# A hybrid recurrent and attention layer: two gate tiles ahead of the pairs, the bias of the first heads in a buffer of its own, the causal mask by GpSimd's select

## The chip, the cores and the metric

The kernel runs on one core of one Trainium2 chip. Its engines are TensorE (PE in the profile, with the weight loads as PEld), VectorE (DVE), ScalarE (ACT), GpSimd (POOL) and SyncE (SP), which only issues transfers. Each takes its own instructions in order and waits on semaphores for the others. The metric is the device time of one execution in microseconds (us); lower is better.

## The reference

One layer of a streaming encoder on 512 tokens of width 1024, all in float32. The part that matters here:

```python
proj = h @ w_in                      # xa, ga, q, k, v, f, gA, gB
y_a = gelu(ga) * rg_lru(conv(xa))    # recurrent branch, width 1280
cum = cumsum(log_sigmoid(f + b_forget))            # one row for each of 16 heads
sc = q @ k.T / 8 + cum[:, None] - cum[None, :]     # in blocks of 128 queries
sc = where(key <= query, sc, -inf)                 # causal mask
y_b = softmax(sc) @ v                              # width 1024
merged = sigmoid(gA + bA) * (y_a @ P_A) + sigmoid(gB + bB) * (y_b @ P_B)
x = x + norm(merged @ w_out)                       # then the feed-forward part
```

The eight column tiles of 128 of `gA` are called ma0 to ma7 in the kernel and those of `gB` mb0 to mb7. The feed-forward part after it (`up` and `dn` in the profile) is not touched by the change.

## The kernel before

Every float32 product is made of three matmuls of rounded parts: each operand is split into a high part, a cast by ScalarE, and a low part, the remainder by VectorE (`wh` and `wl` of a weight, `hh` and `hl` of the normed input, `h_q` and `l_q` of a projection). `mm3` (line 218) issues the three, and `project` (223) makes one tile of 128 output channels by 512 tokens of 24 such matmuls.

The stages stand one behind the other: input norm and `xa`, `v`, the recurrent branch with `ga`, the product `pa` (y_a times P_A), the gates, attention, `pb` (y_b times P_B) with the merge, `wo`, and the feed-forward part. The weights that are fetched one tile at a time stand in the list `order` (186 to 199). `unit(name, ahead)` takes the tile of that name and, ahead of that, emits load (SP's queue), cast and subtraction of all tiles up to `ahead` places behind it. All raw, high and low weight tiles come from one pool with four buffers of each kind (94).

Of the gates, ma0 to ma7 and mb0 to mb5 are made in seven pairs of tiles by a scheme that saves multiplications (`Pair`, 333, and `period`, 431), which needs sums of weight parts (`gt`, `gth`, `gtl`, pool `gsum`), plain parts (`gmh`, `gml`, pools `gsplit0` and `gsplit1`) and kept partial results (`gx`, pool `gkeep`). A low plain part is made by ScalarE's negated copy and an adding transfer from GpSimd's queue (354). mb6 and mb7 are plain projections (`gate_tile`, 869): mb6 stands ahead of the pairs (883), mb7 in attention's last iteration (1071). Each gate's tanh is used at once (ma) or stored to DRAM in `gmb` (mb, 867) and loaded again for the merge.

Attention runs over eight pairs of heads p (1064). An iteration issues, in this order, the scores of pair p, the projection q of pair p + 1, the transposes `pt` of the probabilities of pair p - 1, the projection k of pair p + 1, the halves of q and k, and the product `av` of pair p - 1 with the values; then the division of pair p. In the first iteration there is no `pt` and no `av`; in the last one mb7 stands in the place of q and `pb_part(0, ...)` in that of k. Behind the loop follow `pt` and `av` of the last pair, with parts of pb0, pb1 and pb2 between them (1084 to 1088). `pb_part(e, ks)` adds the steps ks of tile pb e, three matmuls each; step k needs `yb[k]`, the result of `av` of pair k.

The scores of a head need its bias row, which `prep_alloc` (953) fetches: a transfer from GpSimd's queue spreads the row `cnd[h]`, which lies in DRAM since the `pa` stage, over 128 partitions of a tile `B` (957), and two adding transfers put the mask of 128x128, `maskf`, onto its four diagonal blocks (960). VectorE adds scores and bias and takes the extreme of each row (990), ScalarE takes the exponential (995), VectorE divides (1005). `B` has two buffers, one for each head of a pair, so the fetch for pair p + 1 waits until the scores of pair p have been read. `B`, `maskf` and all other tiles of attention lie in the pool `attn`, opened behind the gates over the place of `gsum` and `gkeep`.

PSUM has eight banks (96). The scores of a pair take six, `pt` six, `av` two, every projection and every open pb tile one.

The order of the instructions is the text's between `tc.manual_schedule()` (890) and the end of the gates' block. Elsewhere a planner with estimated times may issue a later instruction first when an earlier one would wait. Memory is taken over from closed pools; with `reuse_waits="tile"` an instruction waits only for the old tiles under its own.

Of the kernel before, what the change touches and what calls it, by code (L numbers as in the profile page):

```python
# [63 lines left out]
def kernel(  # L64
# [115 lines left out]
    def cols(w, i):  # L180
        return w[i], (KD, P)
# [7 lines left out]
    order += [(f"pa{e}_{i}", w_pa[2 * e + i], (5, P)) for e, i in PA_ORDER]  # L189
    order.append(("mb6", *cols(w_in, B_MB + 6)))  # L190
    for p in range(KD):
        order.append((f"q{p}", *cols(w_in, B_Q + p)))
        order.append((f"k{p}", *cols(w_in, B_K + p)))
    order.append(("mb7", *cols(w_in, B_MB + 7)))
    order += [(f"pb{e}", *cols(w_pb, e)) for e in range(KD)]
# [276 lines left out]
    with ExitStack() as rg:  # L472
# [336 lines left out]
        dstk = mstk.enter_context(ExitStack())  # L809
        hfstk = ExitStack()  # L810
        fq = []

        def early_sums(step):
            if step == 3:
                forget()
                rg2.close()
                gates.tpool = dstk.enter_context(tc.tile_pool(name="gsum", bufs=2, reuse_waits="tile"))
                gates.kpool = dstk.enter_context(tc.tile_pool(name="gkeep", bufs=2, reuse_waits="tile"))
                hfpool = hfstk.enter_context(tc.tile_pool(name="hf", bufs=1, reuse_waits="tile"))
                fq.extend(hfpool.tile([P, KH, SH], F32, name=f"hf{i}") for i in range(4))  # L820
            elif 6 <= step < 10:
                i = step - 6
                k, c = (slice(0, KH), slice(KH, KD))[i % 2], (X, Y)[i // 2]
                dve.tensor_tensor(out=fq[i], in0=hh[:, k, c].bitcast(F32), in1=hl[:, k, c].bitcast(F32), op=ALU.add)
            elif step == 10:
                dve.tensor_tensor(out=fq[3], in0=fq[2], in1=fq[3], op=ALU.add)
                sub(fq[2], fq[0], fq[2])
            elif step == 11:
                sub(fq[0], fq[3], fq[0])
                sub(fq[1], fq[1], fq[0])  # L830
            elif step == 12:
                gp[0] = Pair(gates, 0, GP[0])
            elif step == 13:
                gp[0].sums(0)
                gp[0].sums(1)
            elif step == 14:
                gp[0].sums_hi(0)
                gp[0].sums_lo(0)
            elif step == 15:
                gp[0].sums_hi(1)  # L840
                gp[0].sums_lo(1)
# [40 lines left out]

    gate_tile("mb6", 0)
    with ExitStack() as g2:
# [9 lines left out]
        hfstk.close()  # L894
        st0pool = g2.enter_context(tc.tile_pool(name="gsplit0", bufs=2, side="right", reuse_waits="tile"))
        offset(g2, 448, "right")
        st1pool = g2.enter_context(tc.tile_pool(name="gsplit1", bufs=2, side="right", reuse_waits="tile"))
        gates.stpools = [st0pool, st1pool]
# [27 lines left out]
        for j in range(len(GP)):  # L926
            period(gp[j], gp.get(j - 1), gp.get(j + 1, none), gp.get(j + 2, none), gate_epilogue, lambda: more(j))
            gp.pop(j - 1, None)
        b = gp.pop(len(GP) - 1)
        b.add(b.c[:, Y], b.a[:, Y], 1)  # L930
# [9 lines left out]
        gate_epilogue(b, "a", 1)  # L940
    dstk.close()

    with ExitStack() as at:
        apool = at.enter_context(tc.tile_pool(name="attn", bufs=2, reuse_waits="tile"))

        maskf = apool.tile([P, P], F32, name="maskf", bufs=1)
        pool.memset(maskf, 0.0)
        pool.affine_select(
            out=maskf, in_=maskf, compare_op=ALU.is_ge, fill=NEG, base=0,
            pattern=[[-1, P]], channel_multiplier=1)  # L950
        mask2 = maskf.rearrange("p (a b) -> p a b", a=1).to_broadcast([P, 2, P])

        def prep_alloc(p):
            bias = []
            for h in (2 * p, 2 * p + 1):
                B = apool.tile([P, PO[NT]], F32, tag="B", name=f"B{h}")
                nc.gpsimd.dma_start(B, cnd[h : h + 1, :].partition_broadcast(P))
                for c0, w, o in ((0, 256, 0), (256, 512, 384)):
                    diag = B[:, c0 : c0 + 2 * w].rearrange("p (a b) -> p a b", a=2)[:, :, o : o + P]
                    nc.gpsimd.dma_start(diag, mask2, accum_op=ALU.add)  # L960
                bias.append(B)
            return bias

# [96 lines left out]

        bias = prep_alloc(0)
        q, k = halves(pq, "q0"), halves(pk, "k0")
        prev = None
        for p in range(KD):
# [5 lines left out]
            else:  # L1070
                gate_tile("mb7", 2)
            if prev is not None:
# [5 lines left out]
            else:  # L1078
                pb_part(0, range(KD - 2))
            if prev is not None:  # L1080
# [3 lines left out]
        pts = pt(KD - 1, prev)  # L1084
        pb_part(1, range(KD - 1))
        av(KD - 1, pts)
        pb_part(0, range(KD - 2, KD - 1))
        pb_part(2, range(KD - 1))

# [10 lines left out]
    def tg_load(e):  # L1100
        if e < KD:
            tgs[e] = tgpool.tile([P, S], F32, tag="tg", name=f"tg{e}")
            nc.sync.dma_start(tgs[e], gmb[e])

    for e in range(2):
        tg_load(e)
# [559 lines left out]
```

## Time and profile before

| what | value |
| --- | --- |
| time, median of 3 runs | 937.4 us (936.6 to 939.69) |
| profiled execution | 937.35 us |
| span of its profile | 935.6 us |
| instructions | 15714 |
| mean granted TensorE clock | 0.994 |
| DMA | 191.27 MB, mean 204 GB/s |

The span runs from the first to the last instruction of the profiled execution; 1.75 us of its time lie around it. A row of a timeline gives start and duration in us, engine, line, operation, the tile written and the tiles read, shapes and count; in brackets the idle time of the engine just ahead of it and what ended that. A row of waits gives engine, tile and line that waited, what it waited for, the total in us, the number of times and the longest. A row of a window gives its bounds, its length, busy time and instructions of TensorE, the granted clock as a share of full speed, the mean busy share of the DMA engines and GB/s. In the names, numbers of buffers are left out: mb6 and mb7 are both `mb`.

### The profile page before, as it was taken

Reading aid. Unit: us, or ns where it says so; the run is one execution under the profiler, and the core shown is the slowest. Engines: PE = TensorE matmul, PEld = TensorE weight load, DVE = VectorE, ACT = ScalarE, POOL = GpSimd, SP = SyncE. Lnnn points to the kernel's source line nnn. Section 1 sums busy time; section 2 is a strip of 40 time slices with the busy share of each in tenths; the row PEclk is TensorE's granted clock in tenths of the full one; section 3 lists DMA queues with packets and bytes.
Section 4 is the critical chain, followed back from the end, with each engine's and each line's share of the span. In section 5 each row is a group of like instructions: output and inputs, shape, how many; then the busy total and the mean of one; then the engine's idle time right before and its main releaser. Section 6 shows DMA issues by size and latency. Waiting matters only on the chain.

```text
span 935.6 us, 15714 instructions
## 1 busy us (share of the span) xinstructions
PE 911.4 (97%) x5834; PEld 803.7 (86%) x5834; DVE 724.7 (77%) x1184; ACT 596.9 (64%) x1033; POOL 243.1 (26%) x252
## 2 busy tenths in 40 slices
PE   8999999999989997999999999999999999999996
PEld 7988888878889985788888889999999999978885
DVE  5866369537967446888876678999999999889897
ACT  7555495433467535677663376687888888676664
POOL 4134335434121123423303200033232323100001
PEclk9999999999999998999999999999999999999999
DMA  7667589989687586757743555088988989699764
GB/s 276 218 224 206 161 233 261 252 212 199 162 213 182 151 256 167 182 147 187 163 180 130 196 180 182 17 201 219 230 231 211 225 223 205 220 367 328 235 205 143
DMA packets 80320, 191.27 MB, mean 204 GB/s; under 512 B 7729, under 2 KB 36193, under 8 KB 79858
## 3 DMA queue, kind: packets, MB, share of 16 engines
q1 hardware_dynamic: 47360, 127.33, 40.8%
q0 software_dynamic: 32592, 62.40, 32.2%
q8 instruction: 46, 0.75, 0.3%
q10 hardware_dynamic: 290, 0.53, 0.1%
q14 instruction: 32, 0.26, 0.1%
HBM read 150.69 MB, written 35.73 MB: 199 GB/s over the span
## 4 chain that ended last, share of the span: by engine, by line
PE 84%; DMA 7%; DVE 3%; issue 3%; POOL 1%; ACT 1%; SPq 0%; DVEq 0%; POOLq 0%; ACTq 0%
PE up L406 6%; PE up L409 6%; PE up L407 6%; PE dn L1390 4%; PE dn L1388 4%; PE dn L1389 4%; DMA B<-maskf 2%; PE ga L221 2%; PE ga L220 2%; PE ga L219 2%; PE pa L220 2%; PE pa L219 2%; PE pa L221 2%; PE pb L219 2%; PE wo L1129 2%
## 5 line engine op out<-in xcount | busy, mean ns | idle before, releaser
L354 POOL DMA_DIRECT2D ml<-raw_up x41 | 35.1, 857 | 158.7 <-ACT mh L362 75.7
L1274 DVE SCALAR_TENSOR_TENSOR u<-up,cpt,u 128x511 f32<-128x511 f32 x96 | 71.2, 744 | 2.6 <-ACT u L1268 0.9
L1390 PE MATMUL dn<-wh_dn,al 128*128 128x512 f32 x168 | 65.7, 391 | 0.8 <-DVE al L318 0.8
L1388 PE MATMUL dn<-wh_dn,ah 128*128 128x512 f32 x168 | 65.5, 390 | 0.1
L1389 PE MATMUL dn<-wl_dn,ah 128*128 128x512 f32 x168 | 65.4, 389 | 0.0
L406 PE MATMUL up<-sh,th 128*128 128x256 f32 x252 | 60.6, 277 | 1.6 <-DVE up L425 1.1
L407 PE MATMUL up<-sl,th 128*128 128x256 f32 x252 | 60.4, 276 | 0.0
L175 DVE TENSOR_TENSOR wl_dn<-raw_dn,wh_dn 128x1024 fp32r<-128x1024 f32 x42 | 51.5, 1226 | 9.3 <-ACT wh_dn L172 9.2
L172 ACT CAST wh_dn<-raw_dn 128x1024 fp32r<-128x1024 f32 x42 | 44.1, 1049 | 17.7 <-issue 11.5
L318 DVE TENSOR_TENSOR tl<-t,th 128x1024 fp32r<-128x1024 f32 x42 | 51.1, 1218 | 2.5 <-ACT th L388 2.5
L1282 POOL TENSOR_TENSOR yf<-u,u 128x512 f32<-128x512 f32 x24 | 32.2, 1341 | 69.4 <-issue 43.5
L406 PEld LDWEIGHTS up<-sh,th 128*128 128x128 f32 x252 | 47.3, 188 | 2.0 <-DVE up L425 1.3
L995 ACT ACTIVATE P<-P,mx 128x384 f32<-128x384 f32 (+2 forms) x64 | 35.2, 552 | 20.7 <-DVE mx L990 19.8
L388 ACT CAST th<-t 128x1024 fp32r<-128x1024 f32 x42 | 43.8, 1044 | 6.3 <-DVE t L318 4.0
L960 POOL DMA_DIRECT2D B<-maskf x32 | 39.2, 1756 | 31.6 <-DMA B<-cnd 31.3
L407 PEld LDWEIGHTS up<-sl,th 128*128 128x128 f32 x252 | 47.3, 188 | 0.0
L1268 ACT ACTIVATE u<-up,cpt 128x512 f32<-128x512 f32 x48 | 37.0, 779 | 16.2 <-PE up L409 8.8
L406 PE MATMUL up<-h2h,mh 128*128 128x256 f32 x168 | 40.2, 276 | 0.0
L407 PE MATMUL up<-h2l,mh 128*128 128x256 f32 x168 | 40.2, 276 | 0.0
L1390 PEld LDWEIGHTS dn<-wh_dn,al 128*128 128x128 f32 x168 | 31.5, 188 | 8.6 <-DVE al L318 2.1
L409 PE MATMUL up<-sh,tl 128*128 128x256 f32 x252 | 38.9, 276 | 0.0
L353 ACT ACTIVATE ml<-raw_up 128x512 fp32r<-128x512 f32 (+1 forms) x41 | 34.2, 833 | 6.6 <-DMA raw_up<-in_w_up_dram 6.6
(718 smaller groups left out, 3275.1 us busy)
## 6 DMA issues: line engine op xcount, KB each, us to landing
raw_up<-in_w_up_dram SPq DMA_DIRECT2D x48, 512.0 KB, 5.4
td<-in_w_down_dram POOLq DMA_DIRECT2D x36, 512.0 KB, 6.1
raw_dn<-td SPq DMA_DIRECT2D x24, 512.0 KB, 5.1
B<-cnd POOLq DMA_DIRECT2D x16, 640.0 KB, 5.1
ml<-raw_up POOLq DMA_DIRECT2D x20, 512.0 KB, 5.2
raw_dn<-in_w_down_dram SPq DMA_DIRECT2D x18, 512.0 KB, 3.7
raw_wo<-in_w_out_dram SPq DMA_DIRECT2D x16, 512.0 KB, 3.6
td<-td POOLq DMA_DIRECT2D x12, 512.0 KB, 10.9
```

The lines of the kernel that those rows point to most:

```text
L172: act.copy(self.wh, self.raw)
L175: engine.tensor_tensor(out=self.wl, in0=self.raw, in1=self.wh.bitcast(F32), op=ALU.subtract)
L219: pe.matmul(dst, ah, bh, start=first, stop=False)
L318: dve.tensor_tensor(out=out, in0=a, in1=b, op=ALU.subtract)
L388: act.copy(self.th[i], self.t[i])
L406: pe.matmul(dst, wh[:, k], ah[:, k], start=first and k == 0, stop=False, skip_group_check=True)
L407: pe.matmul(dst, wh[:, k], al[:, k], start=False, stop=False, skip_group_check=True)
L409: pe.matmul(dst, wl[:, k], ah[:, k], start=False, stop=k == KH - 1, skip_group_check=True)
L1274: dve.scalar_tensor_tensor(out=c[:, s:], in0=ps[:, : S - s], scalar=col(C_CFW + 3 * e + j), in1=c[:, s:], op0=ALU.mult, op1=ALU.add)
L1388: pe.matmul(dst[t], ah[:, k, tok], wh[:, k], start=first, stop=False, skip_group_check=True)
L1389: pe.matmul(dst[t], ah[:, k, tok], wl[:, k], start=False, stop=False, skip_group_check=True)
L1390: pe.matmul(dst[t], al[:, k, tok], wh[:, k], start=False, stop=last, skip_group_check=True)
```

## The change

Four things are changed. mb7 moves in `order` and in the text from attention's last iteration to right behind mb6, ahead of the pairs. The bias tiles get a pool of their own, `bias`, with two buffers, opened behind the pairs' loop in the place of `gsum` (which is now above `gkeep` and closed early, as are the pools of the split parts), and the first pair's `prep_alloc` is issued there, ahead of the last additions, q0 and k0. The mask is no longer a tile added by transfers: GpSimd's `affine_select` puts -1e30 into the upper half of each of the four diagonal blocks of a bias tile, in place. And in the tail pb0's first six steps take mb7's place, pb1's first six those of pb0; the seventh steps of both follow the last `pt`, then pb2's first seven, and then the last `av`. `gkeep` stays open until the merge.

```diff
--- before.py
+++ after.py
@@ -187,11 +187,10 @@
     order += [(f"v{c}_{u}", w_in[B_V + 4 * c + u], (2, 512)) for c in range(2) for u in range(4)]
     order += [(f"ga{t}", *cols(w_in, B_GA + t)) for t in range(TR)]
     order += [(f"pa{e}_{i}", w_pa[2 * e + i], (5, P)) for e, i in PA_ORDER]
-    order.append(("mb6", *cols(w_in, B_MB + 6)))
+    order += [(f"mb{e}", *cols(w_in, B_MB + e)) for e in (6, 7)]
     for p in range(KD):
         order.append((f"q{p}", *cols(w_in, B_Q + p)))
         order.append((f"k{p}", *cols(w_in, B_K + p)))
-    order.append(("mb7", *cols(w_in, B_MB + 7)))
     order += [(f"pb{e}", *cols(w_pb, e)) for e in range(KD)]
     for ph in range(2):
         order += [(f"wo{ph}_{k}", *rows(w_out, k)) for k in range(KD)]
@@ -807,15 +806,15 @@
         GP = [(f"{w}{e}", f"{w}{e + 1}") for w, n in (("ma", 8), ("mb", 6)) for e in range(0, n, 2)]
         gp = {}
         dstk = mstk.enter_context(ExitStack())
-        hfstk = ExitStack()
+        sumstk, hfstk, splitstk, bstk = (ExitStack() for _ in range(4))
         fq = []
 
         def early_sums(step):
             if step == 3:
                 forget()
                 rg2.close()
-                gates.tpool = dstk.enter_context(tc.tile_pool(name="gsum", bufs=2, reuse_waits="tile"))
                 gates.kpool = dstk.enter_context(tc.tile_pool(name="gkeep", bufs=2, reuse_waits="tile"))
+                gates.tpool = sumstk.enter_context(tc.tile_pool(name="gsum", bufs=2, reuse_waits="tile"))
                 hfpool = hfstk.enter_context(tc.tile_pool(name="hf", bufs=1, reuse_waits="tile"))
                 fq.extend(hfpool.tile([P, KH, SH], F32, name=f"hf{i}") for i in range(4))
             elif 6 <= step < 10:
@@ -880,7 +879,21 @@
             else:
                 gate_use(name, b.tg[which])
 
-    gate_tile("mb6", 0)
+    def prep_alloc(p):
+        bias = []
+        for h in (2 * p, 2 * p + 1):
+            B = bpool.tile([P, PO[NT]], F32, tag="B", name=f"B{h}")
+            nc.gpsimd.dma_start(B, cnd[h : h + 1, :].partition_broadcast(P))
+            bias.append(B)
+        for B in bias:
+            for b in (3, 2, 1, 0):
+                diag = B[:, PO[b + 1] - P : PO[b + 1]]
+                pool.affine_select(out=diag, in_=diag, compare_op=ALU.is_ge, fill=NEG, base=0,
+                                   pattern=[[-1, P]], channel_multiplier=1)
+        return bias
+
+    gate_tile("mb6", 1)
+    gate_tile("mb7", 0)
     with ExitStack() as g2:
         spool = g2.enter_context(tc.tile_pool(name="gsums", bufs=1, side="right", reuse_waits="tile"))
         gates.sh = [spool.tile([P, KH, SH], F32R, name=f"gsh{i}") for i in range(4)]
@@ -892,9 +905,9 @@
             act.copy(gates.sh[i], f)
             sub(gates.sl[i], f, gates.sh[i].bitcast(F32))
         hfstk.close()
-        st0pool = g2.enter_context(tc.tile_pool(name="gsplit0", bufs=2, side="right", reuse_waits="tile"))
-        offset(g2, 448, "right")
-        st1pool = g2.enter_context(tc.tile_pool(name="gsplit1", bufs=2, side="right", reuse_waits="tile"))
+        st0pool = splitstk.enter_context(tc.tile_pool(name="gsplit0", bufs=2, side="right", reuse_waits="tile"))
+        offset(splitstk, 448, "right")
+        st1pool = splitstk.enter_context(tc.tile_pool(name="gsplit1", bufs=2, side="right", reuse_waits="tile"))
         gates.stpools = [st0pool, st1pool]
         none = Nothing()
         p, n = gp[0], gp[1]
@@ -926,6 +939,10 @@
         for j in range(len(GP)):
             period(gp[j], gp.get(j - 1), gp.get(j + 1, none), gp.get(j + 2, none), gate_epilogue, lambda: more(j))
             gp.pop(j - 1, None)
+        splitstk.close()
+        sumstk.close()
+        bpool = bstk.enter_context(tc.tile_pool(name="bias", bufs=2, reuse_waits="tile"))
+        bias = prep_alloc(0)
         b = gp.pop(len(GP) - 1)
         b.add(b.c[:, Y], b.a[:, Y], 1)
         b.add(b.c[:, X], b.c[:, X], 0)
@@ -938,28 +955,10 @@
         b.product(4, b.a[:, Y])
         gate_epilogue(b, "a", 0)
         gate_epilogue(b, "a", 1)
-    dstk.close()
 
     with ExitStack() as at:
+        at.enter_context(bstk)
         apool = at.enter_context(tc.tile_pool(name="attn", bufs=2, reuse_waits="tile"))
-
-        maskf = apool.tile([P, P], F32, name="maskf", bufs=1)
-        pool.memset(maskf, 0.0)
-        pool.affine_select(
-            out=maskf, in_=maskf, compare_op=ALU.is_ge, fill=NEG, base=0,
-            pattern=[[-1, P]], channel_multiplier=1)
-        mask2 = maskf.rearrange("p (a b) -> p a b", a=1).to_broadcast([P, 2, P])
-
-        def prep_alloc(p):
-            bias = []
-            for h in (2 * p, 2 * p + 1):
-                B = apool.tile([P, PO[NT]], F32, tag="B", name=f"B{h}")
-                nc.gpsimd.dma_start(B, cnd[h : h + 1, :].partition_broadcast(P))
-                for c0, w, o in ((0, 256, 0), (256, 512, 384)):
-                    diag = B[:, c0 : c0 + 2 * w].rearrange("p (a b) -> p a b", a=2)[:, :, o : o + P]
-                    nc.gpsimd.dma_start(diag, mask2, accum_op=ALU.add)
-                bias.append(B)
-            return bias
 
         def halves(ps, name):
             hi = apool.tile([P, S], F32R, tag=f"{name[0]}h", name=f"h_{name}", bufs=1)
@@ -1058,7 +1057,6 @@
             for k in ks:
                 mm3(pb[e], wh[:, k], wl[:, k], yb[k][:, 0], yb[k][:, 1], k == 0, k == KD - 1)
 
-        bias = prep_alloc(0)
         q, k = halves(pq, "q0"), halves(pk, "k0")
         prev = None
         for p in range(KD):
@@ -1068,7 +1066,7 @@
                 pq = bank(f"q{p + 1}")
                 project(pq, unit(f"q{p + 1}"), hh, hl)
             else:
-                gate_tile("mb7", 2)
+                pb_part(0, range(KD - 2))
             if prev is not None:
                 pts = pt(p - 1, prev)
             if p < KD - 1:
@@ -1076,16 +1074,16 @@
                 project(pk, unit(f"k{p + 1}"), hh, hl)
                 q, k = halves(pq, f"q{p + 1}"), halves(pk, f"k{p + 1}")
             else:
-                pb_part(0, range(KD - 2))
+                pb_part(1, range(KD - 2))
             if prev is not None:
                 av(p - 1, pts)
             normalise(now)
             prev = now
         pts = pt(KD - 1, prev)
-        pb_part(1, range(KD - 1))
+        for e in range(2):
+            pb_part(e, range(KD - 2, KD - 1))
+        pb_part(2, range(KD - 1))
         av(KD - 1, pts)
-        pb_part(0, range(KD - 2, KD - 1))
-        pb_part(2, range(KD - 1))
 
     ustk = ExitStack()
     h2pool = ustk.enter_context(tc.tile_pool(name="h2T", bufs=1, side="right", reuse_waits="tile"))
@@ -1102,6 +1100,7 @@
             tgs[e] = tgpool.tile([P, S], F32, tag="tg", name=f"tg{e}")
             nc.sync.dma_start(tgs[e], gmb[e])
 
+    dstk.close()
     for e in range(2):
         tg_load(e)
     for e in range(KD):
```

## Prediction

> **What bounds the kernel now.** I read the page first, the share of each engine:
>
> ```profile
> PE 911.4 (97%) x5834; PEld 803.7 (86%) x5834; DVE 724.7 (77%) x1184; ACT 596.9 (64%) x1033; POOL 243.1 (26%) x252
> ```
>
> TensorE is busy 97% of the span of 935.6 us, so a change that leaves its matmuls as they are can gain at most its idle stretches and the time at a lower clock. The waits of TensorE, longest first, say where these lie:
>
> ```profile
> PE s2c L981 <- ACT h_k L967: 4.5, 1, 4.5
> PE ma L409 <- DMA gml<-raw_ma: 1.7, 1, 1.7
> PE ma L406 <- DVE ma L425: 1.3, 1, 1.3
> PE s4c L981 <- DVE l_k L968: 1.0, 1, 1.0
> PE ma L406 <- ACT gmh L362: 0.4, 1, 0.4
> ```
>
> Two places count. The gates' first pair (the ma rows) waits 0.4 + 1.3 + 1.7 = 3.4 us. Attention's first pairs (the rows s2c and s4c) wait 5.5 us, and more is lost there, since the granted clock falls with the idleness. The windows of TensorE, with granted clock behind the busy time:
>
> ```profile
> 354.00:362.00 8.00, 4.76 (x26) 0.57 0.86 229
> 388.00:475.00 87.00, 87.00 (x643) 1.00 0.66 163
> ```
>
> From 388 to 475 us, the rest of attention, it never idles: nothing is to be gained there. The wait of 4.5 us is put down to ScalarE's cast h_k. The chain of waits says what held that up (start, us, what):
>
> ```profile
> 333.25 13.31 DMA B<-maskf
> ```
>
> and the timelines of GpSimd, VectorE and ScalarE show the order:
>
> ```profile
> 316.99 0.55 POOL L957 DMA_DIRECT2D B<-cnd  x1 [2.68 <-DVE gtl L318]
> 317.55 0.31 POOL L948 TENSOR_SCALAR_AFFINE_SELECT maskf<-maskf 128x128 f32<-128x128 f32 x1
> 331.64 0.57 POOL L957 DMA_DIRECT2D B<-cnd  x1 [13.78 <-DVE mb L425]
> 341.62 1.19 POOL L960 DMA_DIRECT2D B<-maskf  x1 [6.66 <-DMA B<-cnd]
> 346.73 0.69 DVE L990 CUSTOM_DVE_ANT_0 P<-s0c,B 128x512 f32<-128x512 f32 x1 [5.72 <-DMA B<-maskf]
> 356.52 0.58 ACT L967 CAST h_k<-k 128x512 fp32r<-128x512 f32 x1
> ```
>
> The second head's bias is issued only at 331.64, since its buffer overlaps what the gates' last addition reads. The adding transfers of the mask take 13.31 us to land. So VectorE reads the first scores at 346.73, the exponentials follow, and ScalarE, which works in order, casts the next k at 356.52, long after its projection.
>
> **The change part by part.** *mb7 ahead of the pairs.* Attention's iterations, by the starts of their first matmuls:
>
> ```profile
> 341.47 0.50 PE L219 MATMUL q<-hh,wh_q 128*128 128x512 f32 x1
> 382.33 0.50 PE L219 MATMUL q<-hh,wh_q 128*128 128x512 f32 x1
> 399.71 0.50 PE L219 MATMUL q<-hh,wh_q 128*128 128x512 f32 x1
> 405.38 0.28 PE L1017 MATMUL pt<-ident,P 64*128 64x64 f32 x2
> 406.77 0.50 PE L219 MATMUL k<-hh,wh_k 128*128 128x512 f32 x1
> 412.34 0.39 PE L1041 MATMUL av<-PTh,v 128*128 128x512 f32 x1
> 414.91 0.50 PE L981 MATMUL s8c<-h_k,h_q 64*128 64x512 f32 x1
> 417.11 0.50 PE L219 MATMUL q<-hh,wh_q 128*128 128x512 f32 x1
> ```
>
> A projection of 24 matmuls, q here and mb7 in the last iteration, takes 405.38 - 399.71 = 5.67 us. Those of mb7 leave attention and stand behind mb6: nothing in the sum of the matmuls. There they run beside the gates' start:
>
> ```profile
> 259.86 0.37 ACT L413 COPY gx<-ma 128x256 f32<-128x256 f32 x1 [2.02 <-PE ma L409]
> 260.66 0.42 DVE L425 TENSOR_TENSOR ma<-ma,gx 128x256 f32<-128x256 f32 x1
> 258.13 0.69 DVE L318 TENSOR_TENSOR gt<-raw_ma,raw_ma 128x512 f32<-128x512 f32 x1
> 448.20 1.23 DVE L175 TENSOR_TENSOR wl_pb<-raw_pb,wh_pb 128x1024 fp32r<-128x1024 f32 x1 [2.03 <-ACT wh_pb L172]
> ```
>
> The 5.67 us cover the wait for the cast (0.4) and for the gml transfer (1.7) even when mb7's own cast and subtraction (of the form of wl_pb, 1.23) go ahead of them on ScalarE and VectorE. Of the 1.3 the chain matmul, copy (0.37), addition (0.42), matmul stays, some 0.9 with its hand-overs; 0.4 goes, in which VectorE finished a sum first. Gain 0.4 + 1.7 + 0.4 = **2.5 us**, with 1.5 (the moved work collides) and 3.4 (all of it) as ends. mb7's load joins SP's queue between mb6's and the first pair's successors; the four raw buffers then come free one load later for the second raw_ma. It is first read at 258.13, and TensorE needs the result 5.67 us later than now: covered. Its tanh and its store to gmb join ScalarE and SP with the others; behind that store wait the next loads of gate weights, which have as much cover.
>
> *First heads' bias, and the mask by select.* 32 adding transfers, maskf and its two GpSimd instructions go. 64 selects of 128x128 come, eight for each pair, and the first two bias loads are issued in the gates' stage. They lie over the sums' buffers, whose last reader let GpSimd go at 316.99; one may touch a buffer of the plain parts, which the last pair's product 3 reads shortly ahead of q0. The load of 331.64 landed 10 us later, at 341.62. At that rate both land by some 327, and eight selects end well ahead of the first use, 346.73 - 5.72 = 341.0: that wait goes, and with it what follows. The loads share the queues with k0's weights; q0's projection, 5.67 us, covers these. On GpSimd nothing is queued behind the selects but the next bias loads. Attention's other tiles lie 16 KB higher, over splits and sums of the gates that are read for the last time ahead of q0: no wait. The size follows from the starts above. An undisturbed iteration takes 417.11 - 399.71 = 17.40 us, of which pt is 406.77 - 405.38 = 1.39 and av 414.91 - 412.34 = 2.57. The iteration of pair 0 (its q projection starts at 341.47) has neither: 13.44 us. But av is what covers the casts of k in the others:
>
> ```profile
> 447.14 0.39 PE L1041 MATMUL av<-PTh,v 128*128 128x512 f32 x1
> 448.07 0.58 ACT L967 CAST h_k<-k 128x512 fp32r<-128x512 f32 x1
> 449.34 0.68 DVE L968 TENSOR_TENSOR l_k<-k,h_k 128x512 fp32r<-128x512 f32 x1
> ```
>
> From the end of the projection (447.14) h_k takes until 448.65, 1.5 us, and l_k until 450.02, 2.9 us. So a wait remains ahead of pair 1's scores, 1.5 and then 0.6 behind the matmuls that need h_k alone: 2.1 us. Pairs 0 and 1 then take 13.44 + 2.1 + 17.40 = 32.9 us, against 382.33 - 341.47 = 40.86 now. Gain **7.9 us**; 10.0 if independent matmuls fill the remaining wait, 6 if the selects delay pair 1 by some 2 us.
>
> What the selects cost in the other pairs: the only one in the trace took 0.31, beside an idle VectorE. What a GpSimd instruction costs in contention, the small copies show (min/median/max in ns), and what VectorE runs most in attention:
>
> ```profile
> L149 POOL COPY tick<-wh_v x8: 1170/1171/1172, 60.2 to 114.5; 128x1 f32<-128x1 f32 x8
> L149 POOL COPY tick<-wh_xa x5: 178/187/1172, 32.2 to 52.0; 128x1 f32<-128x1 f32 x5
> 390.16 4.88 POOL L960 DMA_DIRECT2D B<-maskf  x4 [3.53 <-DMA B<-cnd]
> 399.79 0.69 DVE L990 CUSTOM_DVE_ANT_0 P<-s7c,B 128x512 f32<-128x512 f32 x1
> ```
>
> The same copy of 128x1 takes 0.19 or 1.17 us: up to 0.98 more when it is held. A select lies between 0.31 and 1.29; I take 0.5, nearer the select's own row. The first bias of a pair has landed at 390.16 and the second is read at 399.79: 9.6 us for eight selects that need 4, in place of adding transfers with their landing. Cost nothing; VectorE loses at most 8 x 0.31 = 2.5 us in an iteration of 17.4.
>
> The Trainium skill speaks against this part: its page "SBUF — State Buffer", section "Who interferes with whom", has GpSimd and VectorE share one pair of ports that is held for a whole instruction, so that a GpSimd instruction that reads SBUF and a VectorE instruction with two SBUF inputs, or in a two-port mode, block each other. By that rule each select may wait for a whole subtraction of attention's weights; the copies' two durations agree with it, and what it would make of the time is the slower rival below.
>
> *pb in the tail.* The same 192 pb matmuls in another order. mb7's place is filled by pb0 (18 matmuls), pb0's by pb1. But pb2 now stands ahead of the last av, and the first matmuls written behind that av need its result:
>
> ```profile
> 358.41 0.79 PE L219 MATMUL q<-hh,wh_q 128*128 128x512 f32 x1
> 483.15 0.28 PE L1017 MATMUL pt<-ident,P 64*128 64x64 f32 x2
> 483.87 0.69 DVE L1046 TENSOR_TENSOR y<-av,ytmp 64x512 f32<-64x512 f32 x1 [0.53 <-ACT ytmp L1045]
> 485.25 0.69 DVE L1049 TENSOR_TENSOR yb<-y,yb 128x512 fp32r<-128x512 f32 x1
> 492.03 0.45 PE L219 MATMUL pb<-yb,wh_pb 128*128 128x512 f32 x1
> 494.23 0.69 DVE L1049 TENSOR_TENSOR yb<-y,yb 128x512 fp32r<-128x512 f32 x1 [0.69 <-ACT yb L1048]
> ```
>
> The last av ends at 492.03 and its yb is there at 494.92: 2.9 us, now covered by 24 pb matmuls. After the change they are covered only if pb3's matmuls, ready and later in the text, are issued first; such a lift happens already (the q matmul of 358.41 stands among pair 1's scores). Ahead of it the last pt needs six banks while pb0, pb1 and av's two are held: the last comes free when y is read (484.56, 1.4 us behind pt's start), about 0.8 us of wait. And pb0's step 6 follows pt at once, where yb comes at 485.94, 2.8 us behind av against pt's 1.46: some 0.5 more. Full price 2.9 + 0.8 + 0.5 = 4.2; nothing if all is lifted; I take **+1.2**.
>
> Sum: -2.5 - 7.9 + 1.2 = -9.2. The profiled execution took 937.35 us, the median is 937.4: **928.2 us**.
>
> **The rivals.** *The tail waits in full*: +4.2 instead of +1.2 gives 931.2. For it: the order of the text; against it: the lifted q matmul. *The first bias comes late all the same* (the change doesn't do what it says): the new buffer waits for another tile or the load lands behind its neighbours. Then pair 0's wait stays, and of attention's gain only pair 1's late part goes: s4c's 1.0, and in the chain one landing of adds; some 3 of 7.9, so 933. Against it: even the load of 331.64, landed at 341.62 without the queue of adds behind it, would beat 346.73. *Selects partly held*, 1.29 each: 8 x 1.29 = 10.3 from 390.16 ends at 400.5, 0.7 late in each of seven iterations, 5 us: 933. *Selects held by every subtraction* (the other side): 0.31 + 1.23 = 1.54 each ends at 390.16 + 12.3 = 402.5, 2.7 us behind the read at 399.79, seven times, 19 us: 947, slower. It decides from about 1.36 us a select, where 8 x 1.36 - 9.6 = 1.3 us an iteration eats the 9.2. Against it: the select's own 0.31, and that an iteration has only two such subtractions.
>
> **How the numbers follow.** Forecast 0.57 (its own range 924 to 931), tail in full 0.15, late bias 0.05, selects partly held 0.07; two of these together, some 936, 0.07; selects held throughout 0.09. A measurement of this kernel tells about 0.3%, 2.8 us, from no change: faster 0.84, same 0.07, slower 0.09. The range reaches from all gains at their upper ends (3.4 + 10.0, no cost: 924, and 0.5 for the scatter) to the first four cases with their scatter: 923.5 to 935.
>
> **What would show it.** Right: no wait at ma rows but about 0.9; h_k of pair 1 within 2 us of its projection; clock 1.00 from 354 to 362; the s8c to q marks still 17.4 apart. Wrong: selects above 1.2 us, a wait of VectorE on them in the later pairs, TensorE idle behind the last av, or a wait ahead of k0's projection since the early bias loads share the queues with its weights.

## The result and the profile after

The changed kernel takes 925.43 us (median of 4 runs, 924.3 to 925.92), the kernel before 937.0 (936.49 to 939.69) beside it: a ratio of 0.9869, with a 95% interval of 0.9848 to 0.9891. The page of its profile begins:

```profile
span 923.2 us, 15775 instructions
PE 907.4 (98%) x5834; PEld 802.3 (87%) x5834; DVE 722.3 (78%) x1184; ACT 598.3 (65%) x1033; POOL 222.0 (24%) x282
```

The matmuls are as many as before; the span is 12.4 us shorter (935.6 - 923.2), of which TensorE is busy 4.0 us less and idle 8.4 us less. The waits of TensorE that answer to those of the prediction:

```profile
...
PE s2c L980 <- ACT h_k L966: 1.4, 1, 1.4
PE ma L405 <- DVE ma L424: 0.9, 1, 0.9
...
PE pt L1016 <- DVE y L1045: 0.4, 1, 0.4
```

The 4.5 us ahead of pair 1's scores (s2c) are 1.4, those ahead of pair 2's (s4c) are gone, and of the gates' 3.4 us the 0.9 of one chain is left. One wait of 0.4 is new, in the tail. The two windows of before, with busy time and granted clock of TensorE:

```profile
354.00:362.00 8.00, 6.61 (x43) 1.00 0.39 138
388.00:475.00 87.00, 87.00 (x644) 1.00 0.40 140
```

The clock in the first is 1.00 where it was 0.57; the second never idled and doesn't now. What the clock is worth shows in the windows from the first matmul of s0c to that of s4c, pairs 0 and 1 of attention, before and after:

```profile
338.56:378.98 40.42, 34.63 (x202) 0.92 0.71 188
```

```profile
341.37:374.50 33.13, 31.15 (x201) 1.00 0.58 201
```

Of the 7.29 us that this stretch gains, 3.81 are idle time (5.79 before, 1.98 after) and 3.48 are busy time, for the same matmuls at a granted clock of 1.00 instead of 0.92: the lower clock cost nearly as much as the waits. To see where the time came from, take from the timelines of TensorE the first matmul of each stage, before:

```profile
254.44 0.28 PE L406 MATMUL ma<-gsh,gth 128*128 128x256 f32 x1
...
326.06 0.39 PE L219 MATMUL q<-hh,wh_q 128*128 128x512 f32 x1
...
338.56 0.50 PE L981 MATMUL s0c<-h_k,h_q 64*128 64x512 f32 x1
...
378.98 0.49 PE L981 MATMUL s4c<-h_k,h_q 64*128 64x512 f32 x1
...
397.51 0.50 PE L981 MATMUL s6c<-h_k,h_q 64*128 64x512 f32 x1
...
467.11 0.50 PE L981 MATMUL s14c<-h_k,h_q 64*128 64x512 f32 x1
...
526.79 0.39 PE L1129 MATMUL wo<-wh_wo,mh 128*128 128x512 f32 x1
```

and after:

```profile
260.71 0.28 PE L405 MATMUL ma<-gsh,gth 128*128 128x256 f32 x1
...
328.87 0.39 PE L218 MATMUL q<-hh,wh_q 128*128 128x512 f32 x1
...
341.37 0.50 PE L980 MATMUL s0c<-h_k,h_q 64*128 64x512 f32 x1
...
374.50 0.50 PE L980 MATMUL s4c<-h_k,h_q 64*128 64x512 f32 x1
...
391.88 0.50 PE L980 MATMUL s6c<-h_k,h_q 64*128 64x512 f32 x1
...
461.42 0.50 PE L980 MATMUL s14c<-h_k,h_q 64*128 64x512 f32 x1
...
516.58 0.39 PE L1128 MATMUL wo<-wh_wo,mh 128*128 128x512 f32 x1
```

Their differences, in us, for these two and for the experiments below (`pa` to `ma` is the stage ahead, into which mb7's projection has gone; `up` to `dn` is the feed-forward part, which no kernel of the table alters):

| profile | pa-ma | ma-q | q-s0c | s0c-s4c | s4c-s6c | s6c-s14c | s14c-wo | up-dn |
| --- | --- | --- | --- | --- | --- | --- | --- | --- |
| before | 63.55 | 71.62 | 12.50 | 40.42 | 18.53 | 69.60 | 59.68 | 237.92 |
| after | 69.02 | 68.16 | 12.50 | 33.13 | 17.38 | 69.54 | 55.16 | 236.33 |
| bias and select alone (e1) | 63.57 | 73.07 | 12.50 | 33.18 | 17.38 | 69.53 | 59.69 | 236.41 |
| gate tile and tail alone (e2) | 68.98 | 68.17 | 12.50 | 40.72 | 18.57 | 69.57 | 56.30 | 236.35 |
| select, bias as before (e4) | 68.99 | 68.16 | 12.50 | 33.20 | 17.38 | 69.55 | 55.17 | 238.21 |
| early bias, mask added (e3b) | 69.08 | 68.20 | 16.48 | 33.18 | 17.96 | 69.55 | 55.14 | 236.89 |
| each select three times (e5) | 69.02 | 68.32 | 12.50 | 36.72 | 17.38 | 69.88 | 55.19 | 236.45 |
| each select six times (e6) | 68.99 | 68.27 | 12.51 | 37.31 | 27.53 | 96.13 | 61.65 | 236.31 |
| three steps of q2 first (e7) | 69.07 | 68.16 | 12.50 | 31.64 | 17.42 | 69.52 | 55.20 | 236.55 |
| after, with the old tail (e8) | 69.00 | 68.18 | 12.57 | 33.14 | 17.37 | 69.46 | 55.52 | 236.36 |

From before to after: gates -3.46, attention's start -7.29 and -1.15, mb7 leaving attention and entering the gates, with the tail, 5.47 - 4.52 = +0.95. That is -10.95 of the 12.4. The rest is in stages that the change doesn't touch: -1.59 from `up` to `dn` (which varies from 236.3 to 238.2 over the table), +0.80 ahead of `pa`, and -0.66 in sum elsewhere.

The timelines of GpSimd, VectorE and ScalarE show how attention starts now:

```profile
319.80 0.55 POOL L886 DMA_DIRECT2D B<-cnd  x1 [6.86 <-DVE gtl L317]
327.52 0.55 POOL L886 DMA_DIRECT2D B<-cnd  x1 [7.17 <-PE mb L406]
...
333.47 1.03 POOL L891 TENSOR_SCALAR_AFFINE_SELECT B<-B 128x128 f32<-128x128 f32 x4 [4.36 <-DMA B<-cnd]
...
343.74 0.68 DVE L989 CUSTOM_DVE_ANT_0 P<-s0c,B 128x512 f32<-128x512 f32 x1
...
355.26 1.04 ACT L172 CAST wh_k<-raw_k 128x1024 fp32r<-128x1024 f32 x1 [3.58 <-PE k L219]
356.22 0.58 ACT L966 CAST h_k<-k 128x512 fp32r<-128x512 f32 x1
```

The second bias load waits for product 3 (327.52, TensorE's read of a plain part) and has landed 5.95 us after its issue; its selects end at 334.5, 9.2 us ahead of VectorE's first read at 343.74, ahead of which VectorE doesn't idle. The next k's projection ends at 355.46 (its last matmul starts at 355.07 and takes 0.39), but ScalarE has begun to cast a tile of weights, wh_k, at 355.26, and h_k starts behind that, 0.76 us after the projection's end. So up to half of the 1.4 us that are left ahead of s2c go to that cast.

### The profile page after: what moved, and what is told of

Read it like the earlier page. It is cut to its first block, busy times and chain, and to the rows that moved or that the text cites. A ratio compares the mean times of both kernels' runs of the same rounds, so it can differ in the third digit from the quotient of the medians.

```text
span 923.2 us, 15775 instructions
## 1 busy us (share of the span) xinstructions
PE 907.4 (98%) x5834; PEld 802.3 (87%) x5834; DVE 722.3 (78%) x1184; ACT 598.3 (65%) x1033; POOL 222.0 (24%) x282
## 4 chain that ended last, share of the span: by engine, by line
PE 92%; DMA 2%; DVE 2%; issue 1%; ACT 1%; SPq 1%; POOL 0%; DVEq 0%; ACTq 0%; POOLq 0%
PE up L408 7%; PE up L406 7%; PE up L405 7%; PE dn L1389 4%; PE dn L1388 4%; PE dn L1387 4%; PE pa L218 2%; PE ga L219 2%; PE ga L218 2%; PE pa L220 2%; PE pa L219 2%; PE ga L220 2%; PE q L218 2%; PE k L218 2%; PE pb L218 2%; PE wo L1128 2%
## 5 line engine op out<-in xcount | busy, mean ns | idle before, releaser
L1388 PEld LDWEIGHTS dn<-wl_dn,ah 128*128 128x128 f32 x168 | 31.5, 188 | 6.5
L1387 PEld LDWEIGHTS dn<-wh_dn,ah 128*128 128x128 f32 x168 | 31.5, 188 | 6.5
```

Of the source, the lines that this page charges most:

```text
L1387: pe.matmul(dst[t], ah[:, k, tok], wh[:, k], start=first, stop=False, skip_group_check=True)
L1388: pe.matmul(dst[t], ah[:, k, tok], wl[:, k], start=False, stop=False, skip_group_check=True)
```

## The experiments

**e1: bias and select alone.** The order of weights, mb7 and the tail are as before:

```diff
-    order += [(f"mb{e}", *cols(w_in, B_MB + e)) for e in (6, 7)]
+    order.append(("mb6", *cols(w_in, B_MB + 6)))
...
+    order.append(("mb7", *cols(w_in, B_MB + 7)))
...
-                pb_part(0, range(KD - 2))
+                gate_tile("mb7", 2)
```

> The bias part alone: early bias tiles in their own buffer and the select, with mb7 and the tail as before. Theory (the gains of the parts add): only attention's start gains, 8.4 us by the marks of the two profiles, so some 928.6 us; the waits of the first ma pair stay (0.4, 1.3 and 1.7 us), the wait ahead of s2c is about 1.4 us instead of 4.5, and there is no wait at the last pt. Rival (the bias was late because the moved tile gave it no time, so the parts need each other): the wait ahead of s2c stays above 3 us and the time above 932.

Measured: 928.21 us (926.86 to 928.91), ratio 0.9914 (0.9889 to 0.9938). Attention's start gains what it does in the whole change (33.18 and 17.38), and the gates keep their waits. More than that: in this run the clock fell there. The waits of TensorE in the gates, and its windows:

```profile
PE ma L409 <- DMA gml<-raw_ma: 1.8, 1, 1.8
PE ma L406 <- DVE ma L425: 1.3, 1, 1.3
```

```profile
262.00:270.00 8.00, 6.23 (x44) 0.85 1.00 198
270.00:280.00 10.00, 10.00 (x85) 0.95 0.80 244
```

and the first of these windows in the profile of before:

```profile
262.00:270.00 8.00, 6.25 (x54) 1.00 0.99 191
```

The granted clock, 1.00 in both windows in the profile of before with the same waits, is 0.85 and 0.95 here, and the stage takes 73.07 where before took 71.62. So an idle stretch costs its own length in one execution and 1.45 us more in another.

**e2: gate tile and tail alone.** Bias, mask tile and adding transfers are as before; the rest is the change.

> mb7 ahead of the pairs and the changed tail alone, bias and mask as before. Theory: 3.4 us gained at the first ma pair, about 0.9 us lost in the tail, so 934.5 us; the waits ahead of s2c (4.5 us) and s4c (1.0 us) stay as before. Rival (the parts need each other): the wait ahead of s2c shrinks as well and the time falls below 931.

Measured: 935.41 us (933.87 to 936.72), ratio 0.9993 (0.9978 to 1.0008), which can't be told from no change. The gates gain their 3.45 (68.17), and the waits of attention are there still, 5.9 us now ahead of s2c and 1.0 ahead of s4c, with a new one of 0.3 us for a yb in the tail:

```profile
PE s2c L981 <- ACT h_k L967: 5.9, 1, 5.9
...
```

The tail takes 56.30 here, 1.14 more than in the whole change, and so gives back a third of the gates' gain. Its median is 7.2 us above that of e1: attention's start is the larger part of the change.

**e4: the select without the early fetch.** The bias tiles lie in attention's pool again and are fetched where they were; only the mask is made by selects (mb7 and the tail as changed).

> The changed kernel, but the bias tiles lie in attention's pool again, over the gates' kept results, and the first pair is fetched where it was before; the mask by selects. Theory: the second bias of pair 0 is issued some 334 us into the span, lands by 343 to 345 and needs 1 us of selects, just at the first use (343.7 and 344.4): at most 1 us is lost, 925.4 to 926.5 us, so the buffer of its own is worth little beside the select. Rival (the early fetch is what counts): 930 us or more, with a wait of VectorE on B above 3 us in pair 0.

Measured: 926.92 us (926.47 to 927.04), ratio 0.9901 (0.9878 to 0.9923): attention's start as after (33.20 and 17.38), and the 1.5 us over the changed kernel stand in the feed-forward part (238.21 for 236.33). But the run tests less than it was meant to. GpSimd's timeline:

```profile
321.57 0.55 POOL L950 DMA_DIRECT2D B<-cnd  x1 [1.44 <-DVE mb L424]
```

The second bias load goes out at 321.57, not at 331.64 as before. With `maskf` gone from the head of the pool the tiles lie elsewhere, and the load waits for an earlier addition. So a pool of its own isn't needed for an early fetch here, and what a late one costs with selects isn't shown.

**e3 and e3b: the early fetch without the select.** The bias is fetched early and the mask is put on by the adding transfers. In e3 the mask tile lay in the pool of constants:

```diff
-    cpool.tile([P, 120], F32, name="offset0")
+    maskf = cpool.tile([P, P], F32, name="maskf")
...
-    offset(mstk, 96)
+    offset(mstk, 64)
```

> The changed kernel, but the mask is put on by the adding transfers of before: the first pair's bias is fetched early, no selects. Theory (the landing of the adds is half of the loss): pair 0 no longer waits, pair 1's bias still lands late, VectorE waits for it and the casts of the next q and k stand behind the exponentials; some 3 us of the 8.4 are lost, 929 us, with waits of VectorE on B of several us in pair 1 and little in pair 0. Rival A (the early fetch is the whole gain): 925.4 us and no wait of TensorE beyond those of the changed kernel. Rival B (the select is the whole gain): 933 us or more.

Measured: 946.03 us (943.7 to 948.35), ratio 1.0106 (1.0076 to 1.0136), slower than before, and than the changed kernel in nearly every stage: `up` to `dn` took 243.27 us. That can't be the bias; e9 below, with selects and the same shift of tiles, takes 944.51. Against e9, e3 tests the adding transfers alone, and they cost little: TensorE's wait ahead of s2c is 1.4 us in both, and the 1.45 us more from s0c to s4c (35.21 for 33.76) are a lower clock behind that wait in this execution (0.86 from 360 to 370 us, where e9 has 1.00 from 357 to 367). e3b is the same with the mask tile in the pool of the kept partial results (`gkeep`), all other tiles in their places.

> The early fetch with the adding transfers once more, with the mask tile in a buffer of the gates' kept results, so that no other tile moves. Theory (after the shifted run, whose attention lost about 1.6 us in pair 1 beyond its slower matmuls): pair 0 no longer waits, pair 1 does for its adds, 1 to 2 us are lost against the changed kernel, 926.5 to 927.5 us. So either half of the bias part alone would be nearly enough. Rival (the select is the whole gain): 933 us or more.

Measured: 930.1 us (927.99 to 930.67), ratio 0.9917 (0.9893 to 0.994), some 3 us over what was expected, and in another place. Pairs 0 and 1 lose nothing (33.18), pair 2 loses 0.58, and 3.98 us go at k0's projection (q to s0c: 16.48). The timelines of GpSimd and ScalarE there, and a row of TensorE's waits:

```profile
325.63 0.57 POOL L886 DMA_DIRECT2D B<-cnd  x1
327.68 0.55 POOL L886 DMA_DIRECT2D B<-cnd  x1 [1.48 <-PE mb L406]
...
334.81 1.04 ACT L172 CAST wh_k<-raw_k 128x1024 fp32r<-128x1024 f32 x1 [7.58 <-DMA raw_k<-in_w_in_dram]
```

```profile
PE k L218 <- ACT wh_k L172: 1.3, 1, 1.3
```

The mask tile's own place held the first bias load back by 5.8 us (325.63 for 319.80), so both loads go out while k0's weights are on their way, and these are cast at 334.81, where ScalarE cast them at 331.15 after the change; TensorE waits 1.3 us for the cast and 0.5 for the low part behind it. The rest of the 3.98 us is a lower clock:

```profile
336.00:341.00 5.00, 4.47 (x12) 0.66 1.15 319
```

This is the collision that the prediction named ("the early bias loads share the queues with its weights"). Which of the transfers delays the weights, e3 indicates. There the first bias load goes out at 327.99, k0's weights at 335.66, and the first adds right behind them:

```profile
336.52 2.48 POOL L891 DMA_DIRECT2D B<-maskf  x2 [0.30 <-issue]
...
339.82 1.05 ACT L172 CAST wh_k<-raw_k 128x1024 fp32r<-128x1024 f32 x1 [4.60 <-DMA raw_k<-in_w_in_dram]
```

The cast follows the issue of these weights by 4.16 us in e3, by 4.81 in e9 without adds, and by 7.14 in e3b, where the first bias load goes out 2.0 us ahead of the weights and the adds only 5.4 us behind them. So it is the late bias load that fits, and not the adds; no run moves the load alone.

**e5 and e6: three and six times as many selects.** Each select is issued n times; the result is the same.

```diff
-                pool.affine_select(out=diag, in_=diag, compare_op=ALU.is_ge, fill=NEG, base=0,
-                                   pattern=[[-1, P]], channel_multiplier=1)
+                for _ in range(3):
+                    pool.affine_select(out=diag, in_=diag, compare_op=ALU.is_ge, fill=NEG, base=0,
+                                       pattern=[[-1, P]], channel_multiplier=1)
```

> The changed kernel with each select issued three times (the second and third change nothing in the values). Theory (a select costs GpSimd's 0.3 us and nobody waits): 24 selects take about 8 us, less than the 9.6 us between landing and use, so 925.4 us within 1 us and no wait of VectorE on B in the later pairs. Rival (port sharing: each select also holds VectorE up): at least 16 x 0.3 us more for VectorE in an iteration, TensorE begins to wait ahead of the scores, 935 us or more.

> The changed kernel with each select issued six times. Theory: 48 selects take 14 to 17 us against 9.6 us of cover, so the bias of each pair is 4 to 7 us late, VectorE waits for it, and part of that reaches TensorE: 940 to 975 us, with waits of VectorE on B in every pair. Rival (much slack in the softmax, which is used a whole iteration later): no change, 926 us.

Measured: e5 929.81 us (929.22 to 931.41), ratio 0.992 (0.9898 to 0.9943), a miss by 4; e6 971.69 us (971.09 to 973.52), ratio 1.0369 (1.0341 to 1.0397), within what the selects' sum let expect. The selects of the changed kernel (min/median/max in ns):

```profile
L891 POOL TENSOR_SCALAR_AFFINE_SELECT B<-B x64: 282/292/1274, 328.1 to 457.7; 128x128 f32<-128x128 f32 x64
```

A select takes 0.29 us, and 1.27 when held. The prediction asked how long a subtraction holds a select; what cost most of the time is the reverse. The low part of k's weights on VectorE, after the change, in e5 and in e6:

```profile
356.34 1.23 DVE L175 TENSOR_TENSOR wl_k<-raw_k,wh_k 128x1024 fp32r<-128x1024 f32 x1 [3.28 <-ACT wh_k L172]
```

```profile
356.35 3.30 DVE L175 TENSOR_TENSOR wl_k<-raw_k,wh_k 128x1024 fp32r<-128x1024 f32 x1 [3.28 <-ACT wh_k L172]
```

```profile
403.71 5.33 DVE L175 TENSOR_TENSOR wl_k<-raw_k,wh_k 128x1024 fp32r<-128x1024 f32 x1 [1.95 <-ACT wh_k L172]
```

In e5 GpSimd is busy with 24 selects when the subtraction is issued; it takes 3.30 us instead of 1.23, l_k behind it is 2.07 us late (359.57 for 357.50), and TensorE waits 2.0 for it:

```profile
PE s2c L981 <- DVE l_k L968: 2.0, 1, 2.0
```

The other 1.6 us of the 3.59 that e5 loses from s0c to s4c come with a lower clock (0.83 from 356 to 366 us). In e6 TensorE waits so from pair 2 on, longest here, and VectorE waits for late selects, as expected for every pair, only in pairs 0 and 1:

```profile
PE s4c L981 <- DVE l_k L968: 7.6, 1, 7.6
...
DVE P L990 <- POOL B L892: 9.2, 5, 4.1
```

Here too the clock falls (0.80 from 380 to 410 us).

This is the rule that the prediction weighed, the Trainium skill's page "SBUF — State Buffer", section "Who interferes with whom": a VectorE instruction with two SBUF inputs and a GpSimd instruction that reads SBUF exclude each other. The trace agrees on both sides: a select of 1.27 us (0.29) beside a subtraction, and subtractions of 3.30 and 5.33 (1.23) beside a row of selects. Both of these end some 1.1 us behind the last select of their row (358.57 and 407.97), as if they had run only when the whole row was done. But not every subtraction is held so long: in e6, one of q's weights ran beside the selects that began at 395.13 and took 1.35.

```profile
396.62 1.35 DVE L175 TENSOR_TENSOR wl_q<-raw_q,wh_q 128x1024 fp32r<-128x1024 f32 x1 [2.21 <-ACT wh_q L172]
```

What decides which of the two waits isn't shown. The softmax reads, with one input from PSUM, keep their time (0.69).

**e7: cover for the wait that is left.** The 1.4 us ahead of s2c remain since the first iteration has no `av`. Three steps of q2's projection are written ahead of pair 1's scores:

```diff
+            lead = 3 if p == 1 else 0
+            if lead:
+                pq = bank(f"q{p + 1}")
+                wq = unit(f"q{p + 1}")
+                steps(range(lead))
             now = scores(p, q, k, bias)
```

> The changed kernel, with the first three steps of the projection q2 (9 matmuls, 2.0 us) written ahead of pair 1's scores. Theory: they fill the wait of 1.4 us for the cast h_k, so 1.4 us less, 924.0 us, and no wait ahead of s2c. Rival (the steps only displace the two q matmuls that the planner lifts already, and the low part of k is late all the same): 925.4 us.

Measured: 924.1 us (923.31 to 924.58), ratio 0.9856 (0.9835 to 0.9877). The waits of TensorE from 326 to 480 us hold no s2c any more (0.6 ahead of s0c and 0.4 at the last `pt` are all), and s0c to s4c takes 31.64, 1.49 less. In the medians the step from 925.43 is within the intervals; the stage shows it.

**e8 and e10: the old tail.** e8 is the changed kernel with the pb tiles as before and nothing in mb7's place; e10 has that and the lead of e7.

```diff
-            else:
-                pb_part(0, range(KD - 2))
...
-                pb_part(1, range(KD - 2))
+                pb_part(0, range(KD - 2))
...
-        for e in range(2):
-            pb_part(e, range(KD - 2, KD - 1))
-        pb_part(2, range(KD - 1))
+        pb_part(1, range(KD - 1))
         av(KD - 1, pts)
+        pb_part(0, range(KD - 2, KD - 1))
+        pb_part(2, range(KD - 1))
```

> The changed kernel with the tail as before: nothing stands in the place of mb7, pb0's first six steps stand in that of k, pb1's first seven between the last pt and the last av, pb0's seventh and pb2 behind it. The prediction's theory: the changed tail costs about 1 us (from the first matmul of s14c to the first of wo: 55.16 us in the changed kernel, 59.68 before less the 5.45 that mb7's projection measured, so 54.23), so with the old one the stage takes 54.2 and the median is 924.5 (925.43 - 0.93). A rival: without any matmuls in the place of mb7, pt of pair 6 follows right behind the scores of pair 7, and its probabilities or its six PSUM banks are not ready: TensorE waits 2 us or more there, the stage takes over 56 us, and the new order of the pb tiles was the better one for a kernel without mb7 in the last iteration.

> Both: the old tail, and the first three steps of q2's projection written ahead of pair 1's scores. If the two are independent, the gain of the lead (1.5 us in the stage from s0c to s4c: 33.13 to 31.64) adds to that of the tail: 923.0 where the tail gains 0.93, and about 926 where the rival holds in the tail (2 us lost there).

Measured: e8 925.91 us (924.8 to 929.17), ratio 0.9887 (0.9866 to 0.9908); e10 924.94 us (923.86 to 927.03), ratio 0.9876 (0.9854 to 0.9897). The theory falls: the tail takes 55.52, not 54.2. e8's waits there:

```profile
PE pt L1016 <- DVE mx L989: 0.6, 1, 0.6
...
```

`pt` of pair 6 now follows the scores of pair 7 at once and needs PSUM banks that VectorE is still reading. The rival named this wait, at 2 us or more and over 56 in all; it is 0.8 (0.6 and 0.2 more for its second part), and the stage lies between the two. So the new order costs nothing against the old one once mb7 is gone: it is 0.36 better in the stage, which the medians don't resolve. In e10 the two are independent, as both theories had it: 31.78 in s0c to s4c, and 55.55 in the tail.

**e9: 32 bytes.** e3's slowdown in nearly all stages came with a tile of 512 bytes in place of one of 480, which shifts what lies behind it by 32 bytes. e9 is the changed kernel with three paddings altered, so that the pools of weight tiles and small tiles lie shifted by 32 bytes and all else stays:

```diff
-    cpool.tile([P, 120], F32, name="offset0")
+    cpool.tile([P, 128], F32, name="offset0")
...
-    offset(mstk, 96)
+    offset(mstk, 64)
...
-    offset(fstk, 96)
+    offset(fstk, 64)
```

> The changed kernel in which three paddings are altered, so that the weight tiles and the small tiles lie 32 bytes lower and all else stays: the computation is the same. Two theories on why the run with mask tile and early fetch took 946 us, 16 us more than the same kernel with the mask tile in another pool. Placement: the 32 bytes alone slow the matmuls that read these tiles, 389 to 396 ns for those of the down product and 277 to 283 for those of up, and the median is 925.4 + 15.9 = 941, between 938 and 944. Transfers: the slowdown came with the adding transfers or the mask tile itself; then this run takes 925.4 within 1.5 us, with matmuls of 389 and 277 ns.

Measured: 944.51 us (943.92 to 944.81), ratio 1.0079 (1.0056 to 1.0101): 19 us over the changed kernel, half a microsecond above the placement theory's bounds, and far from the other's. Groups of matmuls of the down product (mean ns) in the changed kernel and in e9:

```profile
L1388 PE MATMUL dn<-wl_dn,ah 128*128 128x512 f32 x168 | 65.4, 389 | 0.0
```

```profile
L1388 PE MATMUL dn<-wl_dn,ah 128*128 128x512 f32 x168 | 66.4, 395 | 0.0
```

and those of `up` in e9 (min/median/max in ns):

```profile
L405 PE MATMUL up<-h2h,mh x168: 276/276/283, 607.4 to 805.8; 128*128 128x256 f32 x168
L405 PE MATMUL up<-h2h,th x84: 279/283/283, 622.1 to 818.6; 128*128 128x256 f32 x84
```

The second row reads `th`, which lies in the shifted pool, the first `mh`, which doesn't, and the other operand is the same: 283 ns against 276 (in the changed kernel both take 276). Adding transfers and mask tile are out as causes of nearly all of it. But not every matmul with weights from the shifted pool is slower. In the gates, gth lies in the same pool, and the median there is 281 ns in the changed kernel and 280 in e9:

```profile
L405 PE MATMUL ma<-gsh,gth x48: 276/281/385, 260.7 to 301.6; 128*128 128x256 f32 x48
```

```profile
L405 PE MATMUL ma<-gsh,gth x48: 277/280/386, 266.2 to 307.1; 128*128 128x256 f32 x48
```

From `ma` to q, e9 takes 68.13 us, the changed kernel 68.16. So the place of the weight tile isn't the whole rule; what else counts isn't shown.

## Why the prediction was right

The forecast of 928.2 us is 2.8 above what was measured, and the range and the sign held. Step by step:

- *Gates' start.* Taken as 2.5; measured 3.46. The three idle times of before, 0.4 + 1.3 + 1.7, less the 0.9 that stayed, make the 2.5: the mechanism and the wait left were right. The other 0.9 is busy time of the stage (68.12 us before, 67.23 after), which the table of waits doesn't count. Some 0.5 of it lies between two of the stops: 24 matmuls took 3.42 us there before, and 36 in a row take 4.40 after the change (0.142 against 0.122 each). The upper end, 3.4, was closer.
- *mb7 moved.* Taken as neutral at 5.67. Its stage grew by 5.47 (69.02 - 63.55), so 0.2 was gained; why isn't shown.
- *Attention's start.* Taken as 7.9; measured 7.29 + 1.15 = 8.44. The chain was as read: the late bias, the late first read, the late cast h_k; e1 shows it alone. That both halves of the bias part are needed is not shown: with the early fetch and the adding transfers kept, pairs 0 and 1 take 33.18 in e3b, as with selects, and no run has selects with a late fetch. Of the remaining wait ahead of pair 1's scores, put at 1.5 and 0.6, the first measured 1.4 (of which up to 0.76 is the cast of wh_k ahead of it), and the second was filled by two lifted q matmuls.
- *Selects.* Taken as 0.5 us at no cost; 0.29 each and no cost (17.38 for an iteration, 17.40 before). Both outer rivals rested on selects held by subtractions; e5 shows that in the later pairs three times the work nearly fits (69.88 for 69.54 from s6c to s14c). The prediction had the loss begin where a pair's eight selects fill the 9.6 us of cover, at 1.2 us each, through a late first read, and eat the whole gain at 1.36. A loss is there earlier and elsewhere: in e5, with 24 selects in 5.92 us, in pair 1, through VectorE's subtraction.
- *Tail.* Taken as 1.2 on top of mb7's removal: 59.68 - 5.67 = 54.01, measured 55.16, so 1.15. The size was right in part by luck: 1.2 was a choice between nothing and the full price, and only one of the three prices was paid. They were 2.9 (the last yb), 0.8 (the sixth bank of `pt`) and 0.5 (pb0's step 6). The bank was read rightly: from the start of the last `pt` to the pb matmul behind it 2.23 us pass (476.08 to 478.31), 1.47 before (483.15 to 484.62), 0.76 more, of which 0.45 is idle time. The other 0.39 lies elsewhere in the stretch and isn't explained; for step 6 no wait is shown. And the 2.9 cost nothing: the last yb ends at 490.10 (the first row below, VectorE's timeline), TensorE is busy from 487 on without a gap (the second, a window of it), so matmuls that need no last yb were issued there; by the order of the text they are pb3's. e8 shows that the term isn't a price of the new order as against the old: without mb7 in the last iteration the old order pays more (55.52).

```profile
489.41 0.69 DVE L1048 TENSOR_TENSOR yb<-y,yb 128x512 fp32r<-128x512 f32 x1 [0.69 <-ACT yb L1047]
```

```profile
487.00:491.00 4.00, 4.00 (x21) 1.00 0.00 0
```

- *The sum.* -3.46 - 0.20 - 8.44 + 1.15 = -10.95 against -9.2, and 1.45 more of the span in untouched stages, of which the forecast could know nothing (the two profiled executions differ by 12.3 us, the medians by 11.6). Most of the 1.75 is the gates' 0.9 and attention's 0.5.
- *The rivals.* No late bias, no held selects, no tail in full. The collision at k0 did not come in the changed kernel (q to s0c is 12.50 in both), but it came in e3b, as soon as the bias loads went out later.

What stays open: what late bias loads cost together with selects; what decides whether a subtraction waits for a whole row of selects; why the same wait lowers the clock in one execution and not in another; and in which way the 32 bytes act on TensorE.

## What to carry to other kernels

Read a late cast back to the transfer that held up its engine: here the largest wait of TensorE, put down to a cast, went with an earlier fetch of a bias, whichever way its mask was put on. Where work on GpSimd replaces transfers, ask not only whether it is done in time but which VectorE instruction with two SBUF inputs it will stand beside. And when a variant is slower in every stage, compare the mean of one matmul first: a moved tile may be nearly all there is.

## What the runs showed of the hardware

With the pools of weight tiles and small tiles shifted by 32 bytes, matmuls of the down product that read such weights take 395 ns for 389 (128x512) and those of `up` 283 for 276 (128x256), in all 19 us or 2% of the kernel, with no longer wait of TensorE to show it; those of the gates keep their 280 or 281. A VectorE subtraction with both inputs in SBUF took 3.30 and 5.33 us for 1.23 beside rows of selects on GpSimd, and 1.35 beside another such row. And the same idle stretches in the gates left the granted clock at 1.00 in the profile of before and at 0.85 and then 0.95 in e1, 1.45 us of difference with the same waits in that stage; the same 1.4 us ahead of s2c left it at 1.00 in e9 and at 0.86 in e3.
